# Attention scores of a hybrid decoder layer: the low product on 64 rows, two of them in two row tiles of TensorE

## The chip, the cores and the metric

The kernel runs on one core of a Trainium2 chip. A core has five engines with queues of their own: TensorE (PE in the profile; its weight loads are shown apart as PEld), VectorE (DVE), ScalarE (ACT), GpSimd (POOL) and SyncE (SP), which here only issues DMAs. TensorE multiplies a stationary operand of up to 128 rows and 128 columns with a moving operand of up to 512 columns, sums over the rows, and writes to PSUM, a memory of eight banks, each holding 512 numbers of four bytes in each of 128 partitions. The metric is the time of one execution on the device in microseconds (us), as the median of several runs.

## The reference, cut to what matters

One decoder layer over 1024 positions and 1024 channels: a norm, one wide projection, two attentions side by side, a gated merge, then a feed-forward part with a short convolution, and a last norm. The change touches only the scores of the two attentions.

```python
# differential attention: 4 heads, two score maps (c = 0, 1) of head dimension 64, causal, blocks of 128 queries
s = einsum('bqhcd,bshcd->bhcqs', q_blk, k) * scale
logits = where(dist >= 0, s - slope * dist, NEG_INF)
p = softmax(logits)
a = p[:, :, 0] - lam * p[:, :, 1]
# sliding window: 8 query heads on 2 key heads of dimension 64, a block of 128 queries sees 256 keys
s = einsum('bnqkgd,bnskd->bnkgqs', qb, kw) * d ** -0.5
p = softmax(concatenate([logits, sink], -1))[..., :-1]
```

## The kernel before, in words

All matrix products run in a rounded 32-bit type. To keep the accuracy, an operand is split into a high part (rounded) and a low part (the rest), and a product is the sum of partial products of the parts.

For the scores the head dimension is 64, half of TensorE's 128 rows, and the kernel uses the free half for the split. `q_stacks` puts q's high part and q's low part of one head on top of each other in one tile of 128 rows: the high part stands in rows 0 to 63 when c is 0, and in rows 64 to 127 when c is 1 (in the sliding window, for even and odd heads). `k_stack` makes two tiles, one with k's high part in both halves and one with k's low part in both halves. One matmul over 128 rows with the first gives high times high plus low times high; a second one, with the other tile, gives high times low plus low times low. The second is called the low product below.

The attentions are worked through in 6 units (`attention`): 4 heads of the differential attention and 2 key heads of the sliding window, each in 8 steps of 128 queries.

A differential step (`da_step`, L623 to L655) has two halves, c = 0 and 1. Each takes a score tile `sc` of two PSUM banks from a pool of two such tiles, fills it with matmuls (L636; one or two cuts of 256 to 512 keys, each with two products), and then VectorE adds the distance bias and takes the row's extreme (L640), which reads the score tile for the last time, and ScalarE takes the exponential (L641). After both halves VectorE combines the two maps (L646), TensorE transposes the result (L652), ScalarE and VectorE split it (L654, L655), and after every second step TensorE multiplies it with the values (L664 to L666).

A sliding-window step (`sw_step`) fills one `sc` tile with the scores of four heads, 256 keys each (L724): heads 0 and 1 in the tile's first bank, 2 and 3 in its second. VectorE adds the bias for each head (L727); exponentials, transposes (L745) and the product with the values (L755) follow.

Between the steps stand pieces of the wide projection that have nothing to do with attention (`back_half`: 24 matmuls of 512 columns in `mm3`, L209 to L211), placed by a table. The order on each engine isn't the order of the text: a planner goes through the program and issues, on each engine, the earliest instruction in the text whose inputs and buffers are free by its own estimate. An instruction that waits for a buffer is passed over by later ones that are ready. The order is fixed when the program is built; on the chip each engine works through its own list and waits on semaphores.

The places that the change touches are the matmul loop of `da_step` (L630 to L636) and in `sw_step` the matmul loop and the VectorE loop (L722 to L727).

Of the kernel before, what the change touches and what calls it, by code (L numbers as in the profile page):

```python
# [13 lines left out]
ALU = mybir.AluOpType  # L14
# [3 lines left out]
P = 128  # L18
D = 1024
T = 1024  # L20
# [24 lines left out]
class Trunk:  # L45
# [576 lines left out]
    def da_step(self, h, i, st, aT):  # L622
        nc, ap = self.nc, self.ap  # L623
        q, k = st
        slope = 4.0 ** -(h + 1)
        w = (i + 1) * P

        lo = P if w == 640 else 0
        cuts = ((0, 256),) if i == 0 else ((0, w),) if w <= H2 else ((0, H2 - lo), (H2 - lo, w))
        pr = []  # L630
        for c in range(2):
            sc = self.tl(self.psS, [P, T], "sc")
            qs = q[c][:, i * P:(i + 1) * P]
            for part in range(2):
                for n0, n1 in cuts:
                    nc.tensor.matmul(sc[:, lo + n0:lo + n1], qs, k[c][part][:, n0:n1], start=part == 0, stop=part == 1)  # L636
            L = self.tl(ap, [P, T], "L", bufs=4)
            s = self.tl(self.st, [P, 4], "sm", bufs=8)
            o = 896 - i * P
            nc.vector.tensor_tensor_reduce(L[:, :w], sc[:, lo:lo + w], self.bias[:, o:o + w], slope, 3e38, ALU.add, ALU.min, s[:, 0:1])  # L640
            nc.scalar.activation(L[:, :w], L[:, :w], AF.Exp, bias=s[:, 0:1], scale=-1.0, accum_out=s[:, 1:2] if c else self.s0[:, i:i + 1])  # L641
            pr.append(L)

        nc.vector.reciprocal(s[:, 2:3], s[:, 1:2])
        nc.vector.tensor_scalar(s[:, 3:4], self.s0[:, i:i + 1], s[:, 2:3], self.neglam, ALU.mult, ALU.mult)
        nc.vector.scalar_tensor_tensor(pr[0][:, :w], pr[1][:, :w], s[:, 3:4], pr[0][:, :w], ALU.mult, ALU.add)  # L646
        qo = (i % 2) * P
        for j0 in range(0, i + 1, 4):
            nj = min(4, i + 1 - j0)
            ps = self.tl(self.psT, [P, 4, P], "t")  # L650
            for j in range(nj):
                nc.tensor.transpose(ps[:, j, :], pr[0][:, (j0 + j) * P:(j0 + j + 1) * P], self.ident)  # L652
            hi, lo = aT[j0 // 4, 0], aT[j0 // 4, 1]
            nc.scalar.copy(hi[:, :nj, qo:qo + P], ps[:, :nj, :])  # L654
            nc.vector.tensor_tensor(lo[:, :nj, qo:qo + P], ps[:, :nj, :], hi[:, :nj, qo:qo + P].bitcast(F32), ALU.subtract)  # L655
# [57 lines left out]
    def sw_step(self, g, n, st):  # L713
        nc, ap = self.nc, self.ap
        q, k = st
        k0 = max(n - 1, 0) * P
        w = P if n == 0 else 256
        bo = T + (P if n == 0 else 0)
        sc = self.tl(self.psS, [P, 4, 256], "sc")
        s = self.tl(self.st, [P, 4, 4], "sw", bufs=4)  # L720
        L = self.tl(ap, [P, 4, 256], "L", bufs=4)
        for h in range(4):  # L722
            for part in range(2):
                nc.tensor.matmul(sc[:, h, :], q[h][:, n * P:(n + 1) * P], k[part][:, k0:k0 + 256], start=part == 0, stop=part == 1)  # L724
        for h in range(4):
            slope = 2.0 ** -(4 * g + h + 1)
            nc.vector.tensor_tensor_reduce(L[:, h, :w], sc[:, h, :w], self.bias[:, bo:bo + w], slope, 3e38, ALU.add, ALU.min, s[:, 0, h:h + 1])  # L727
        sink = self.vecs[:, C_SINK + 4 * g:C_SINK + 4 * g + 4]
        nc.vector.tensor_tensor(s[:, 0, :], s[:, 0, :], self.nsink[:, 4 * g:4 * g + 4], ALU.min)
        nc.vector.tensor_tensor(s[:, 1, :], s[:, 0, :], sink, ALU.add)  # L730
        nc.scalar.activation(s[:, 1, :], s[:, 1, :], AF.Exp)
        for h in range(4):
            nc.scalar.activation(L[:, h, :w], L[:, h, :w], AF.Exp, bias=s[:, 0, h:h + 1], scale=-1.0, accum_out=s[:, 2, h:h + 1])
        nc.vector.tensor_tensor(s[:, 2, :], s[:, 2, :], s[:, 1, :], ALU.add)
        self.last = nc.vector.reciprocal(s[:, 3, :], s[:, 2, :])
        for h in range(4):
            eng = nc.gpsimd if h in (3,) else nc.vector
            eng.tensor_scalar(L[:, h, :w], L[:, h, :w], s[:, 3, h:h + 1], None, ALU.mult)
        po = self.tl(self.psT, [P, H2], "t")
        nblk = w // P  # L740
        parts = []
        for b in range(nblk):
            ps = self.tl(self.psT, [P, 4, P], "t")
            for h in range(4):
                nc.tensor.transpose(ps[:, h, :], L[:, h, b * P:(b + 1) * P], self.ident)  # L745
            pt = self.tl(ap, [P, 2, 4, P], "aT", F32R, bufs=5)
            hi, lo = pt[:, 0], pt[:, 1]
            nc.scalar.copy(hi, ps)
            nc.vector.tensor_tensor(lo, ps, hi.bitcast(F32), ALU.subtract)
            parts.append((hi, lo))  # L750
        for b, (hi, lo) in enumerate(parts):
            kb = k0 // P + b
            va = self.vsw[kb // 4][:, kb % 4, g]
            for m, pt in enumerate((hi, lo)):
                nc.tensor.matmul(po, va, pt, start=b == 0 and m == 0, stop=b == nblk - 1 and m == 1)  # L755
        t = self.tl(self.gpool, [P, 4, P], "g", bufs=2)[0:64]
        nc.scalar.copy(t, po[64:128].rearrange("p (h q) -> p h q", h=4))
        pv = po[0:64].rearrange("p (c e q) -> p c e q", c=2, e=2)
        tv = t.rearrange("p (c e) q -> p c e q", e=2)
        y = self.tl(ap, [P, 2, P], "ys", bufs=3)  # L760
        for e in range(2):
            nc.vector.tensor_tensor(y[64 * e:64 * e + 64], pv[:, :, e], tv[:, :, e], ALU.add)
        self.store(self.yd[4 + 2 * g:6 + 2 * g, :, n * P:(n + 1) * P].rearrange("c p q -> p c q"), y)
# [683 lines left out]
```

## Time and profile before

| | |
|---|---|
| median of 3 runs | 1341.69 us (1340.93 to 1343.33) |
| the profiled execution | 1342.84 us, of which its span is 1340.6 us |
| mean granted TensorE clock | 0.997 |
| TensorE busy | 1319.9 us in 6264 matmuls |
| TensorE weight loads | 1097.0 us in 6264 loads |
| VectorE busy | 1069.3 us |
| ScalarE busy | 621.2 us |
| score matmuls of the differential attention (L636) | 192, from 256.9 to 390.3 us |
| score matmuls of the sliding window (L724) | 128, from 390.8 to 480.8 us |

In the profile a row of the timeline is: start, duration, engine, line, operation, output and inputs by the program's names, the part of TensorE's array (128*128 is all of it), output shape, how many in a row, and in brackets how long the engine stood idle before and what ended that. A group's row ends with its busy time, the mean duration of one in ns, and the idle time before its members. In the row of a line, three durations are the least, the median and the largest. Records of matmuls overlap: a matmul's record runs until its last result is written, and the next one starts earlier.

### The profile page before, as it was taken

How to read it: one execution, taken by the hardware profiler on the slowest of the kernel's cores; microseconds unless marked ns; L12 is line 12 of the kernel's file. 1: busy time of each engine (PE TensorE's matmuls, PEld its weight loads, DVE VectorE, ACT ScalarE, POOL GpSimd, SP SyncE). 2: the span in 40 equal slices, each digit the busy share in tenths (PEclk: the TensorE clock that was granted, in tenths of full speed). 3: DMA queues.
4: the chain of work that ended last, by engine and by line, in shares of the span. 5: the costliest groups of instructions: out<-in, count | busy, mean ns of one | idle time of the engine just before them, and what ended most of it. 6: DMA issues, size and time to landing. Idle time of an engine off the chain costs nothing.

```text
span 1340.6 us, 17301 instructions
## 1 busy us (share of the span) xinstructions
PE 1319.9 (98%) x6264; PEld 1097.0 (82%) x6264; DVE 1069.3 (80%) x1605; ACT 621.2 (46%) x1019; POOL 497.0 (37%) x365
## 2 busy tenths in 40 slices
PE   8999999999999999999999999999999999999997
PEld 6888888888888777878888888888888888888787
DVE  8847775289889876465678999999999997978985
ACT  9432232276667765333444443444443444323454
POOL 0336553001102124651446555655565510215422
PEclk9999999999999999999999999999999999999998
DMA  7423443876553235334432222222222229671333
GB/s 258 145 107 143 156 158 141 246 182 186 144 135 124 97 119 203 141 110 157 126 110 95 78 95 79 94 68 90 90 85 80 85 82 337 214 263 63 112 124 126
DMA packets 63045, 182.64 MB, mean 136 GB/s; under 512 B 6896, under 2 KB 15216, under 8 KB 62960
## 3 DMA queue, kind: packets, MB, share of 16 engines
q1 hardware_dynamic: 51504, 164.13, 37.5%
q10 hardware_dynamic: 11456, 17.41, 3.6%
q8 instruction: 49, 0.80, 0.3%
q14 instruction: 36, 0.29, 0.1%
HBM read 130.66 MB, written 50.86 MB: 135 GB/s over the span
## 4 chain that ended last, share of the span: by engine, by line
PE 87%; POOL 4%; DVE 4%; DMA 3%; ACT 1%; issue 1%; POOLq 0%; SPq 0%; ACTq 0%; DVEq 0%
PE t L920 13%; PE t L921 13%; PE t L922 13%; PE g L209 3%; PE t L914 3%; PE g L210 3%; PE g L211 3%; PE sc L636 3%; PE y L1159 2%; PE d L1159 2%; DMA gr<-gd 2%; PE sc L211 2%; PE sc L209 2%; PE sc L210 2%; PE d L920 2%; PE d L921 2%
## 5 line engine op out<-in xcount | busy, mean ns | idle before, releaser
L1089 ACT ACTIVATE c<-us,vecs 128x512 f32<-128x512 f32 x80 | 61.3, 780 | 133.2 <-POOL us L1083 129.2
L1091 DVE SCALAR_TENSOR_TENSOR c<-us,vecs,c 128x512 f32<-128x512 f32 x160 | 110.4, 747 | 8.6 <-ACT c L1089 8.5
L1083 POOL TENSOR_TENSOR us<-us,rstd 128x1024 f32<-128x1024 f32 x38 | 99.7, 2643 | 4.5 <-DVE us L469 2.4
L128 DVE TENSOR_TENSOR sl<-sf,sh 128x1024 fp32r<-128x1024 f32 x62 | 87.6, 1415 | 11.5 <-ACT sh L127 11.5
L127 ACT CAST sh<-sf 128x1024 fp32r<-128x1024 f32 x62 | 63.3, 1048 | 60.2 <-PE t L921 43.7
L176 DVE TENSOR_TENSOR wl<-raw,wh 128x1024 fp32r<-128x1024 f32 (+2 forms) x46 | 55.7, 1210 | 31.8 <-ACT wh L174 20.2
L128 DVE TENSOR_TENSOR wl<-raw,wh 128x1024 fp32r<-128x1024 f32 (+1 forms) x35 | 76.3, 2180 | 3.7 <-ACT wh L127 3.6
L103 POOL TENSOR_TENSOR sf<-rv 128x512 f32<-128x512 f32 x30 | 41.3, 1378 | 100.9 <-DVE sl L128 57.8
L174 ACT CAST wh<-raw 128x1024 fp32r<-128x1024 f32 (+2 forms) x46 | 46.1, 1001 | 61.8 <-PE sc L210 30.5
L209 PE MATMUL g<-xh,wh 128*128 128x512 f32 x176 | 70.6, 401 | 0.1
L211 PE MATMUL g<-xh,wl 128*128 128x512 f32 x176 | 70.3, 400 | 0.0
L210 PE MATMUL g<-xl,wh 128*128 128x512 f32 x176 | 70.3, 399 | 0.0
L108 POOL TENSOR_TENSOR sf<-raw,rv 128x512 f32<-128x512 f32 x30 | 40.7, 1358 | 65.3 <-DVE sl L128 65.3
L619 POOL MEMSET aT<- 128x128 f32 x32 | 6.2, 206 | 151.6 <-PE t L665 101.3
L640 DVE CUSTOM_DVE_ANT_0 L<-sc,bias 128x128 f32<-128x128 f32 (+7 forms) x64 | 47.7, 751 | 17.0 <-PE sc L636 13.7
L641 ACT ACTIVATE L<-L,sm 128x128 f32<-128x128 f32 (+7 forms) x64 | 49.6, 778 | 20.0 <-DVE sm L640 17.3
L794 POOL TENSOR_TENSOR gr<-gr,rstd 128x1024 f32<-128x1024 f32 x16 | 40.6, 2540 | 42.5 <-DMA gr<-gd 42.3
L1093 ACT ACTIVATE c<-c 128x512 f32<-128x512 f32 x40 | 24.0, 599 | 60.7 <-DVE c L1091 60.7
L128 DVE TENSOR_TENSOR wl<-rv,wh 128x512 fp32r<-128x512 f32 x30 | 49.3, 1642 | 3.5 <-ACT wh L127 3.5
L636 PE MATMUL sc<-u,u 128*128 128x512 f32 (+2 forms) x192 | 49.8, 358 | 0.0
L211 PE MATMUL sc<-mh,wl 128*128 128x512 f32 x126 | 49.1, 390 | 0.5 <-DVE wl L176 0.5
L209 PE MATMUL sc<-mh,wh 128*128 128x512 f32 x126 | 49.0, 389 | 0.0
(527 smaller groups left out, 4400.3 us busy)
## 6 DMA issues: line engine op xcount, KB each, us to landing
u<-qd SPq DMA_DIRECT2D x72, 256.0 KB, 6.6
raw<-in_w_in SPq DMA_DIRECT2D x25, 512.0 KB, 4.2
raw<-in_w_up SPq DMA_DIRECT2D x23, 512.0 KB, 3.5
hr<-hd SPq DMA_DIRECT2D x46, 256.0 KB, 4.9
hd<-c SPq DMA_DIRECT2D x22, 512.0 KB, 2.6
rv<-in_w_up SPq DMA_DIRECT2D x21, 512.0 KB, 3.5
raw<-in_w_down SPq DMA_DIRECT2D x19, 512.0 KB, 4.2
gr<-gd SPq DMA_DIRECT2D x16, 512.0 KB, 3.7
```

Of the source, the lines that this page charges most:

```text
L127: i = nc.scalar.copy(hi, src)
L128: j = nc.vector.tensor_tensor(lo, src, hi.bitcast(F32), ALU.subtract)
L209: nc.tensor.matmul(ps, wh[:, kc + o, :], ah, start=first and n == 0, stop=False)
L210: nc.tensor.matmul(ps, wh[:, kc + o, :], al, start=False, stop=False)
L211: nc.tensor.matmul(ps, wl[:, kc + o, :], ah, start=False, stop=last and n == len(kcs) - 1)
L636: nc.tensor.matmul(sc[:, lo + n0:lo + n1], qs, k[c][part][:, n0:n1], start=part == 0, stop=part == 1)
L920: nc.tensor.matmul(ps, ah[:, k, :], bh, start=first and n == 0, stop=False, skip_group_check=skip)
L921: nc.tensor.matmul(ps, ah[:, k, :], bl, start=False, stop=False, skip_group_check=skip)
L922: i = nc.tensor.matmul(ps, al[:, k, :], bh, start=False, stop=last and n == len(ks) - 1, skip_group_check=skip)
L1083: (nc.vector if j == 0 else nc.gpsimd).tensor_tensor(u[:, 2:], u[:, 2:], self.rstd, ALU.mult)
L1089: nc.scalar.activation(c, u[:, o + 2:o + 2 + H2], AF.Identity, bias=self.vecs[:, C_CB + m:C_CB + m + 1], scale=col(m, 2))
L1091: nc.vector.scalar_tensor_tensor(c, u[:, o + k:o + k + H2], col(m, k), c, ALU.mult, ALU.add)
```

## The change

In both attentions the low product is taken over 64 rows only: q's high part times k's low part. Low times low is left out of the sum. The high part of c = 0 (or of an even head) stands in rows 0 to 63 and that of c = 1 (or an odd head) in rows 64 to 127, so the two low products use different halves of TensorE's rows, its row tiles; they are written one behind the other, into different PSUM banks.

For this the order of the text changes. A differential step takes both score tiles first, then writes the high products of both halves, then the low products, cut by cut, alternating between the halves; L640 and what follows come after all of them. A sliding-window step writes the high products of its four heads in the order 0, 2, 1, 3, then the low products in the order 0, 1, 2, 3. Heads 0 and 2 now share the first bank and 1 and 3 the second. Since two sums are open in one bank at once, only the first matmul of a bank carries the start flag. The number of matmuls, their columns and the work of the other engines stay as they are.

```diff
-        for c in range(2):
-            sc = self.tl(self.psS, [P, T], "sc")
-            qs = q[c][:, i * P:(i + 1) * P]
-            for part in range(2):
-                for n0, n1 in cuts:
-                    nc.tensor.matmul(sc[:, lo + n0:lo + n1], qs, k[c][part][:, n0:n1], start=part == 0, stop=part == 1)
+        scs = [self.tl(self.psS, [P, T], "sc") for _ in range(2)]
+        for c, sc in enumerate(scs):
+            for n0, n1 in cuts:
+                nc.tensor.matmul(sc[:, lo + n0:lo + n1], q[c][:, i * P:(i + 1) * P], k[c][0][:, n0:n1], start=True, stop=False)
+        for n0, n1 in cuts:
+            for c, sc in enumerate(scs):
+                rows = slice(64 * c, 64 * c + 64)
+                nc.tensor.matmul(sc[:, lo + n0:lo + n1], q[c][rows, i * P:(i + 1) * P], k[c][1][rows, n0:n1], start=False, stop=True)
+        for c, sc in enumerate(scs):
             L = self.tl(ap, [P, T], "L", bufs=4)
...
+        at = lambda h: sc[:, 2 * (h % 2) + h // 2]
+        for h in (0, 2, 1, 3):
+            nc.tensor.matmul(at(h), q[h][:, n * P:(n + 1) * P], k[0][:, k0:k0 + 256], start=h < 2, stop=False, skip_group_check=True)
         for h in range(4):
-            for part in range(2):
-                nc.tensor.matmul(sc[:, h, :], q[h][:, n * P:(n + 1) * P], k[part][:, k0:k0 + 256], start=part == 0, stop=part == 1)
+            rows = slice(64 * (h % 2), 64 * (h % 2) + 64)
+            nc.tensor.matmul(at(h), q[h][rows, n * P:(n + 1) * P], k[1][rows, k0:k0 + 256], start=False, stop=h > 1, skip_group_check=True)
...
-            nc.vector.tensor_tensor_reduce(L[:, h, :w], sc[:, h, :w], self.bias[:, bo:bo + w], slope, 3e38, ALU.add, ALU.min, s[:, 0, h:h + 1])
+            nc.vector.tensor_tensor_reduce(L[:, h, :w], at(h)[:, :w], self.bias[:, bo:bo + w], slope, 3e38, ALU.add, ALU.min, s[:, 0, h:h + 1])
```

## The prediction

> **What bounds the kernel now.** I read the profile's page first, then the busy time of three stretches, then the groups of matmuls in the stretch of the first attention, and then TensorE's timeline row by row, because the change is about which matmul stands beside which. From the page, the span, two engines and the chain that ended last:
>
> ```profile
> span 1340.6 us, 17301 instructions
> ...
> PE 1319.9 (98%) x6264; PEld 1097.0 (82%) x6264; DVE 1069.3 (80%) x1605; ACT 621.2 (46%) x1019; POOL 497.0 (37%) x365
> ...
> PE 87%; POOL 4%; DVE 4%; DMA 3%; ACT 1%; issue 1%; POOLq 0%; SPq 0%; ACTq 0%; DVEq 0%
> ```
>
> TensorE is busy for 98% of the span and 87% of the last chain is its work. The stretches are the differential attention's score matmuls (256 to 391 us), the sliding window's (391 to 484 us) and what follows:
>
> ```profile
> core 0: us, PE busy (x) PEld busy (x) DVE busy (x) ACT busy (x) POOL busy (x), PEclk, DMA share, GB/s
> 256.00:391.00 135.00, 134.92 (x832) 117.19 (x831) 110.20 (x288) 88.84 (x209) 10.64 (x32) 1.00 0.62 165
> 391.00:484.00 93.00, 91.92 (x543) 76.55 (x542) 82.23 (x305) 66.51 (x197) 15.70 (x17) 1.00 0.41 121
> ```
>
> In the first, TensorE idles 0.1 of 135 us, at a granted clock of 1.00; in the second 1.1 of 93. VectorE, at 110 and 82 us, is next but has room. So TensorE time added or saved in these stretches moves the end almost one for one: what follows is bound by TensorE too. The matmuls concerned, from the groups of the first stretch and from the line of the second attention's scores:
>
> ```profile
> L209 PE MATMUL g<-xh,wh 128*128 128x512 f32 x72 | 28.9, 401 | 0.0
> L636 PE MATMUL sc<-u,u 128*128 128x512 f32 x80 | 27.6, 409 | 0.0
> L636 PE MATMUL sc<-u,u 128*128 128x256 f32 x64 | 16.9, 299 | 0.0
> L636 PE MATMUL sc<-u,u 128*128 128x384 f32 x48 | 15.3, 352 | 0.0
> ```
>
> ```profile
> L724 PEld LDWEIGHTS sc<-u,u x128: 186/189/217, 390.5 to 480.7; 128*128 128x128 f32 x128
> L724 PE MATMUL sc<-u,u x128: 274/283/382, 390.8 to 480.8; 128*128 128x256 f32 x128
> ```
>
> "128*128" after the operation is the part of the array in use: all of it here.
>
> **What a matmul costs, and what stands beside the scores.** TensorE's timeline around the last block of the third head and the first of the fourth, and VectorE's hold on two of its weight loads:
>
> ```profile
> 351.14 0.39 PE L210 MATMUL g<-xl,wh 128*128 128x512 f32 x1
> 351.37 1.09 PE L636 MATMUL sc<-u,u 128*128 128x512 f32 x4
> 352.29 0.40 PE L211 MATMUL g<-xh,wl 128*128 128x512 f32 x1
> 352.53 1.17 PE L636 MATMUL sc<-u,u 128*128 128x512 f32 x4
> 353.53 0.39 PE L209 MATMUL g<-xh,wh 128*128 128x512 f32 x1
> 353.76 0.39 PE L210 MATMUL g<-xl,wh 128*128 128x512 f32 x1
> ...
> 356.02 0.40 PE L636 MATMUL sc<-u,u 128*128 128x256 f32 x2
> 356.25 0.40 PE L211 MATMUL g<-xh,wl 128*128 128x512 f32 x1
> ...
> 357.19 0.40 PE L209 MATMUL g<-xh,wh 128*128 128x512 f32 x1
> 357.43 0.40 PE L636 MATMUL sc<-u,u 128*128 128x256 f32 x2
> ```
>
> ```profile
> 352.49 0.77 PEld L636 LDWEIGHTS sc<-u,u 128*128 128x128 f32 x4 [0.24 <-DVE sm L640]
> ...
> 355.90 0.31 PEld L636 LDWEIGHTS sc<-u,u 128*128 128x128 f32 x2 [0.16 <-DVE sm L640]
> ```
>
> Three readings. (1) A 512-column matmul is recorded for 0.39 us, but the next starts 0.23 later (353.53 to 353.76), two of 256 take 0.23 together (356.02 to 356.25), so 0.12 each; 384 columns lie between, about 0.175. The spacing goes by columns. (2) So each matmul overlaps the one before by 0.39 - 0.23 = 0.16 us. (3) The two halves of a head (c = 0 and 1, which use the two score buffers) do not stand together: in each of these steps the first pair or four is followed by other work, and the second waits until VectorE's L640 has emptied its buffer.
>
> **The change, part by part.** Nothing is added or taken away in number: 192 and 128 score matmuls with as many weight loads, the same VectorE, ScalarE, POOL and DMA instructions. What changes is the order of the scores and the 64 rows of the low products.
>
> *Order in the differential attention.* The new text puts both high products first and then the two low ones. But the second high product still needs a buffer that VectorE empties later, while the first low product needs only what is there. The planner of this kernel issues whatever is ready; the two rows of waits above show the second half held. Counted over the timeline, the 192 matmuls stand in 77 unbroken runs, and in 31 of the 32 steps the halves are in different runs; the exception begins at 269.83:
>
> ```profile
> 256.93 0.28 PE L636 MATMUL sc<-u,u 128*128 128x256 f32 x1
> ...
> 269.83 1.12 PE L636 MATMUL sc<-u,u 128*128 128x512 f32 x4
> ...
> 389.62 1.09 PE L636 MATMUL sc<-u,u 128*128 128x512 f32 x4
> ```
>
> So I expect the low products of 31 steps to run one half at a time, without a partner in the other row tile: 62 groups, and one pair, 63.
>
> *Order in the sliding window.* One buffer holds all four heads, so a step's matmuls can stand together. They do in 7 of 16 steps, and the 128 stand in 24 runs, from one matmul at 390.77 to eight at 479.89; where not, older work cuts in, as here:
>
> ```profile
> 399.17 1.20 PE L724 MATMUL sc<-u,u 128*128 128x256 f32 x8
> 400.21 0.39 PE L209 MATMUL g<-xh,wh 128*128 128x512 f32 x1
> ...
> 410.64 0.52 PE L724 MATMUL sc<-u,u 128*128 128x256 f32 x3
> 411.00 0.40 PE L755 MATMUL t<-aT,v 128*128 128x512 f32 x1
> ```
>
> At least 16 groups of low products, 79 in all, each with a border to full-array work on either side: 158 borders. If cut-ins split the low parts as they split today's runs, there are some 99 groups (77 + 24 runs, less the few that hold high parts only).
>
> *Gain of a pair.* If two row tiles ran wholly at once, a pair would save one spacing: in the sliding window 32 pairs x 0.12 = 3.8 us; in the differential attention, were all paired, 20 x 0.23 + 12 x 0.175 + 16 x 0.12 = 8.6 us (half of the 80, 48 and 64 matmuls are low products, two to a pair). But each matmul has its own weight load, and loads set their own pace: eight transposes of 128 columns take 0.80 us to the next matmul (row below, next start 399.17), 0.10 each. Two loads in a row thus need 0.20 where two 256-column matmuls need 0.24, which leaves 0.04 a pair. I take that end, since the loads are measured and their running at once is not: 32 x 0.04 = 1.3 us, plus 0.23 for the pair at 269.83: 1.5 us.
>
> ```profile
> 398.37 1.04 PE L652 MATMUL t<-ident,L 128*128 128x128 f32 x8
> ```
>
> [...]
>
> *Price of a border.* No matmul of before uses part of the array, so no row shows a change from 128 rows to 64 and back. Bounds: zero, if it overlaps like any other; no gain, since spacing goes by columns; above, the 0.16 us of overlap lost and the weight load exposed as well. The latter is seen where TensorE had to start afresh after a wait:
>
> ```profile
> 365.15 0.19 PEld L664 LDWEIGHTS t<-aT,v 128*128 128x128 f32 x1 [0.29 <-DVE aT L655]
> ```
>
> ```profile
> 365.15 0.39 PE L664 MATMUL t<-aT,v 128*128 128x256 f32 x1
> 365.38 0.28 PE L665 MATMUL t<-aT,v 128*128 128x256 f32 x1
> ```
>
> The first takes 0.39 instead of 0.28: 0.11 for its load, so at most 0.27 a border. I take 0.16, between these ends: the overlap is recorded only between matmuls of one shape of array, so I expect it to be lost where the shape changes, the weight load still being made ahead as it is everywhere but after a wait. [...]
>
> *Bank order.* In the sliding window, L727 of head 0 used to follow the fourth matmul, and may now follow the seventh, as heads 0 and 2 share a bank: 3 x 0.12 = 0.36 us later in 16 steps, 5.8 us at most. VectorE has 11 us of idle time in that stretch to hide it; I take 0.
>
> *Sum.* 158 x 0.16 = 25.3, less 1.5 for pairs, less the 1.1 us in which TensorE idles in the sliding window and the stall may hide: +22.7 us. The profiled execution took 1342.84 us (2.2 beyond its span), 1.15 above the median of the three runs, 1341.69; the forecast on the median is 1364.4 us. Its own range, from 126 borders (four in five of them, if some steps pair) to 198: 1359 to 1371.
>
> **The rivals.**
> - *Borders cost next to nothing* (0 to 0.06 us), halves unpaired: -1.5 to +8 us, 1340 to 1350. For it: nothing in the trace shows a border. Against it: the 0.16 us overlap is seen only between matmuls of one shape of array.
> - *Pairs run at once and borders are free: faster.* This needs the halves side by side in the differential attention, that is L640 emptying both buffers before the high products. It gives 12.4 us at best; with the loads' pace 20 x 0.23 + 12 x 0.15 + 48 x 0.04 = 8.3; with some hundredths of a microsecond a border, 5: 1329 to 1337. With 48 groups (96 borders) it decides below 12.4 / 96 = 0.13 us a border; unpaired, already 3.8 / 158 = 0.02 us undoes it. Against it stand the 31 separated steps.
> - *Paired, but borders drain:* 96 x 0.16 = 15.4, less 8.3 to 12.4: +3 to +7, about 1347. The change does what it says and still loses.
> - *Drained and reloaded:* 158 x 0.27 = 42.7, less 2.6: +40, 1382; with 198 borders +51, 1393.
>
> **How the numbers follow.** Forecast 0.47; cheap borders 0.18 (half of it within noise, the rest mostly slower); paired and free 0.08; paired and drained 0.10; drained and reloaded 0.17. The range, 1341 to 1392, leaves out the paired and free case, the faster end of cheap borders and the last microseconds of the worst, about 0.14. A measurement of this kernel tells some 0.2% (2.7 us) from no change. Faster by more: 0.08 and 0.02 of cheap borders, 0.10. Within: 0.09 of cheap borders and 0.02 of paired and drained, 0.11. Slower: 0.79.
>
> **What the changed kernel's profile would show.** The low products as rows with 64*128; if step one is right, those of c = 0 and c = 1 apart with L209 to L211 or L652 between, in about 31 of 32 steps. If the price is right, the matmul after a border starts about 0.39 us after a 512-column one and not 0.23, and the first stretch grows by about 63 x 2 x 0.16 = 20 us, the second by 3 to 5, at the same count of matmuls; VectorE's busy time stays at 110 and 82 us. I would be wrong if starts across borders stay 0.23 apart, if paired rows with starts a few ns apart fill the first stretch, or if the time appears as waits of VectorE for scores instead.

## The result, and the profile after

| | before | after |
|---|---|---|
| median of the runs shown together | 1342.51 us (4 runs, 1340.93 to 1346.34) | 1379.05 us (4 runs, 1378.62 to 1384.07) |
| ratio, 95% interval | | 1.0276 (1.0244 to 1.0309) |
| profiled execution, and its span | 1342.84 us, 1340.6 us | 1378.67 us, 1376.6 us |
| start of the last score matmul, differential | 390.3 us | 419.1 us |
| start of the last score matmul, sliding window | 480.8 us | 514.3 us |

The change makes the kernel 36.5 us slower; the forecast was 22.7 slower. The last differential score comes 28.8 us later, the last sliding-window score 33.5 us, the end 36.0 us (span). So most of the loss arises in the first stretch, 4.7 us in the second, and some 2.5 us behind the last score, where nothing was changed; 1.7 of these lie in a stretch of half clock (last section).

From the page of the kernel after: span, two engines, and the chain that ended last.

```profile
span 1376.6 us, 17292 instructions
...
PE 1354.3 (98%) x6264; PEld 1098.0 (80%) x6264; DVE 1076.8 (78%) x1605; ACT 621.5 (45%) x1019; POOL 498.5 (36%) x365
...
PE 93%; DVE 3%; ACT 1%; DMA 1%; POOL 1%; issue 1%; POOLq 0%; ACTq 0%; SPq 0%; DVEq 0%
```

TensorE has as many matmuls and loads as before and is busy 34.4 us longer, which is nearly all of the loss; VectorE is busy 7.5 us longer and its share fell. The time isn't spent waiting for another engine: it is inside TensorE. The view of two stretches (columns as in the prediction: busy time of PE, PEld, DVE, ACT, POOL, granted clock, DMA share, GB/s), cut where after's two attentions end, a little behind the last scores as there:

```profile
256.00:420.00 164.00, 163.90 (x836) 119.96 (x835) 113.80 (x289) 89.39 (x207) 10.61 (x32) 0.98 0.51 137
420.00:515.50 95.50, 93.25 (x528) 72.87 (x527) 79.02 (x293) 64.52 (x191) 15.01 (x17) 1.00 0.39 113
```

The first holds 836 matmuls in 164 us where before had 832 in 135, and TensorE is still recorded busy all the time. Where the time goes is seen only row by row. This is TensorE's timeline of after around one differential step (start, duration, line, part of the array, output shape, how many):

```profile
304.71 0.42 PE L634 MATMUL sc<-u,u 128*128 128x384 f32 x1
305.06 0.44 PE L638 MATMUL sc<-u,u 64*128 64x384 f32 x1
305.43 0.50 PE L211 MATMUL g<-xh,wl 128*128 128x512 f32 x1
305.77 0.34 PE L634 MATMUL sc<-u,u 128*128 128x384 f32 x1
306.03 0.43 PE L638 MATMUL sc<-u,u 64*128 64x384 f32 x1
306.40 0.50 PE L209 MATMUL g<-xh,wh 128*128 128x512 f32 x1
306.74 0.40 PE L634 MATMUL sc<-u,u 128*128 128x512 f32 x1
```

L634 is a high product, L638 a low one ("64*128"). Each low product stands alone between matmuls over all rows, and the two halves are apart, as the prediction had it. Take the low product at 306.03. By columns it would start 0.175 after the high one at 305.77; it starts 0.26 after, so 0.09 late. The matmul behind it would start 0.175 later; it starts 0.37 later, so 0.19 late. That one has 512 columns, and its successor starts 0.34 later and not 0.23, so 0.11 more. Together some 0.39 us for one lonely low product, of two borders. The first matmul after each border is also recorded about 0.1 us longer than its like (0.50 against 0.39, 0.43 against 0.34).

The weight loads of the same stretch show what the 0.1 is:

```profile
304.68 0.19 PEld L634 LDWEIGHTS sc<-u,u 128*128 128x128 f32 x1
305.06 0.18 PEld L638 LDWEIGHTS sc<-u,u 64*128 64x128 f32 x1 [0.19 <-issue]
305.43 0.19 PEld L211 LDWEIGHTS g<-xh,wl 128*128 128x128 f32 x1 [0.19 <-issue]
305.54 0.19 PEld L634 LDWEIGHTS sc<-u,u 128*128 128x128 f32 x1
```

At a border the load starts with its matmul (305.06 and 305.06, 305.43 and 305.43), after an idle time that no engine caused. Away from it the load runs ahead: that of the L634 matmul of 305.77 starts at 305.54. So it is in all of after's trace: at its 186 borders the load starts 0 to 3 ns before its matmul, between two matmuls over all rows 223 ns before it (median). And the columns overlap the matmul before by less than elsewhere: 0.07 us at the two borders above (0.42 - 0.35 and 0.44 - 0.37), against 0.16 in before's rows (0.39 - 0.23).

Where two low products in different row tiles stand together, they start at once, 3 ns apart. From the timeline, one group of the sliding window in after (L727 high, L730 low):

```profile
425.98 0.74 PE L727 MATMUL sc<-u,u 128*128 128x256 f32 x4
426.65 0.50 PE L730 MATMUL sc<-u,u 64*128 64x256 f32 x4
427.08 0.50 PE L211 MATMUL g<-xh,wl 128*128 128x512 f32 x1
427.42 0.39 PE L209 MATMUL g<-xh,wh 128*128 128x512 f32 x1
```

Four low products of 256 columns take 0.43 us to the next start. That is 0.24, two matmuls' worth and not four, and 0.19 more. The records of such a group start 3, 220 and 3 ns apart: two matmuls in two row tiles start together, and so do their weight loads (2 to 5 ns apart in the 36 such places of after, the matmuls 1 to 5). As an estimate, the 220 ns are the 120 of 256 columns and 100 for the first loads, so of the 0.19 some 0.10 stand inside the group and 0.09 behind it.

Counted over the whole program, after has 93 groups of low products: 70 in the differential attention (47 of one matmul, 20 of two, 3 of three) and 23 in the sliding window. In 36 places two neighbours lie in different row tiles; their saved columns are worth 4.8 us. Over the 93 groups the median excess is 93 ns into a group, 191 ns out of it and 105 ns in the matmul behind: 0.39 us a group, 0.195 a border. Summed over all groups, each start counted once, with the excess inside a group and without time at half clock, it is 36.4 us, again 0.39 a group.

### The profile page after: what moved, and what is told of

It is laid out like the page before. It is cut to its first block, busy times and chain, and to the rows that moved or that the text cites. A ratio compares the mean times of both kernels' runs of the same rounds, so it can differ in the third digit from the quotient of the medians.

```text
span 1376.6 us, 17292 instructions
## 1 busy us (share of the span) xinstructions
PE 1354.3 (98%) x6264; PEld 1098.0 (80%) x6264; DVE 1076.8 (78%) x1605; ACT 621.5 (45%) x1019; POOL 498.5 (36%) x365
## 3 DMA queue, kind: packets, MB, share of 16 engines
q1 hardware_dynamic: 51504, 164.13, 36.5%
## 4 chain that ended last, share of the span: by engine, by line
PE 93%; DVE 3%; ACT 1%; DMA 1%; POOL 1%; issue 1%; POOLq 0%; ACTq 0%; SPq 0%; DVEq 0%
PE t L926 12%; PE t L927 12%; PE t L928 12%; PE g L209 4%; PE g L211 4%; PE g L210 4%; PE sc L209 3%; PE sc L211 3%; PE sc L210 3%; PE t L920 3%; PE y L1165 2%; PE d L1165 2%; PE sc L638 2%; PE d L926 2%; PE d L927 2%; PE d L928 2%
## 5 line engine op out<-in xcount | busy, mean ns | idle before, releaser
L176 DVE TENSOR_TENSOR wl<-raw,wh 128x1024 fp32r<-128x1024 f32 (+2 forms) x46 | 59.1, 1285 | 34.4 <-ACT wh L174 22.8
L209 PE MATMUL g<-xh,wh 128*128 128x512 f32 x176 | 73.7, 418 | 0.4 <-ACT g L565 0.4
L211 PE MATMUL g<-xh,wl 128*128 128x512 f32 x176 | 72.6, 412 | 0.0
L643 DVE CUSTOM_DVE_ANT_0 L<-sc,bias 128x128 f32<-128x128 f32 (+7 forms) x64 | 47.7, 753 | 22.1 <-PE sc L638 14.9
L211 PE MATMUL sc<-mh,wl 128*128 128x512 f32 x126 | 49.1, 390 | 0.0
L210 PE MATMUL sc<-ml,wh 128*128 128x512 f32 x126 | 49.0, 389 | 0.0
L209 PE MATMUL sc<-mh,wh 128*128 128x512 f32 x126 | 49.0, 389 | 0.0
```

Source lines behind the costliest of these rows:

```text
L176: self.lo = (eng or nc.vector).tensor_tensor(wl, raw, wh.bitcast(F32), ALU.subtract)
L209: nc.tensor.matmul(ps, wh[:, kc + o, :], ah, start=first and n == 0, stop=False)
L210: nc.tensor.matmul(ps, wh[:, kc + o, :], al, start=False, stop=False)
L211: nc.tensor.matmul(ps, wl[:, kc + o, :], ah, start=False, stop=last and n == len(kcs) - 1)
```

## Theories and experiments

The theory: each group of low products costs about 0.39 us, whatever is in it, because at the change from 128 rows to 64 and back TensorE overlaps the columns less (some 0.09 us each time) and doesn't load the weights ahead (some 0.105); a pair saves the columns of one matmul; the rest is the new order. The rivals: the order does it (halves wait for their buffers, pieces of projection are used up early); a 64-row matmul is itself slow, wherever it stands; VectorE's late release of a score buffer does it, and better pairing would make the change a gain.

Of the kernels below, those with 64 rows leave out low times low as the change does; the ones with 128-row low products add it again. The probes compute nothing that the result uses. Each was compared with the kernel before on the same chip, whose median there was 1342.5 to 1343.9 us.

**The order alone.** After, with both low products over all rows; the order of the text stays.

```diff
-                rows = slice(64 * c, 64 * c + 64)
+                rows = slice(0, P)
...
-            rows = slice(64 * (h % 2), 64 * (h % 2) + 64)
+            rows = slice(0, P)
```

> The order of the changed kernel, with the low products over all 128 rows as before (so low times low is in the sum again). Theory (borders): the time goes at the changes between 128 and 64 rows, about 0.39 us for each group of 64-row matmuls; there are none here, so the time is that of the kernel before, 1342.5 us, 1340 to 1346. Rival (order): the new order makes VectorE get its scores later; then most of the 36.5 us stays, 1370 or more.

Measured: 1349.53 us (1349.15 to 1350.01), +6.3; ratio 1.0045 (1.003 to 1.006). That is above the theory's range and far below the rival's: the order by itself is a minor part of the loss, but not free, as the prediction had it. The stretch from the end of the differential scores to the last product of the sliding window's values, before and then with the order alone:

```profile
390.40:498.00 107.60, 105.89 (x606) 86.36 (x605) 93.35 (x331) 75.02 (x217) 17.61 (x19) 1.00 0.40 115
```

```profile
393.20:502.00 108.80, 104.67 (x601) 85.02 (x600) 91.94 (x331) 74.65 (x217) 16.78 (x19) 1.00 0.39 113
```

TensorE idles 4.1 us there (108.80 less 104.67) instead of 1.7, with five matmuls fewer to do. In the new order the planner issues more of the projection in the first attention: 219 matmuls of L209 to L211 stand there between the first score and the last, against 209 before, and between that and the last score of the sliding window 162 against 172. Pieces that are missing there, when TensorE waits, would explain the idle time; no run shows it by itself.

**The rows alone.** Before's order, half by half, with the low products over 64 rows: 160 low matmuls in 143 groups and no pair.

```diff
+                rows = slice(64 * c, 64 * c + 64) if part else slice(0, P)
-                    nc.tensor.matmul(sc[:, lo + n0:lo + n1], qs, k[c][part][:, n0:n1], start=part == 0, stop=part == 1)
+                    nc.tensor.matmul(sc[:, lo + n0:lo + n1], qs[rows], k[c][part][rows, n0:n1], start=part == 0, stop=part == 1)
...
+                rows = slice(64 * (h % 2), 64 * (h % 2) + 64) if part else slice(0, P)
+                nc.tensor.matmul(at(h), q[h][rows, n * P:(n + 1) * P], k[part][rows, k0:k0 + 256], start=part == 0, stop=part == 1)
```

> The order of the kernel before (high and low product of one score map behind each other), with 64-row low products; in the sliding window the heads' places in the banks are those of the change. TensorE's list has the same 160 matmuls of 64 rows, but in 143 groups instead of 93, and no two row tiles side by side. Theory (borders): 143 x 0.39 = 55.8 us on 1342.5, 1398, 1392 to 1406. Rival (a 64-row matmul costs more by itself, 36.5 us / 160 = 0.23 us each): the same number of them, 1379. Rival (the row tiles side by side get in each other's way): less than the change, below 1370.

Measured: 1402.94 us (1400.46 to 1406.18), +59.7; ratio 1.0446 (1.0423 to 1.0468). With before's order and the same matmuls the loss is larger than with the change, and it goes with the number of groups: 59.7 / 143 = 0.42 us. Neither rival's time, 1379 or below 1370, is near. A step of the sliding window in this kernel, eight matmuls in which 128 and 64 rows alternate:

```profile
429.07 2.55 PE L727 MATMUL sc<-u,u 128*128 128x256 f32 x8
431.55 0.50 PE L210 MATMUL g<-xl,wh 128*128 128x512 f32 x1
```

They take 2.48 us to the next start; before's eight took 1.04 (399.17 to 400.21 in the prediction's row). Seven inner borders and the one behind them at 0.18 each make the difference.

**Forced pairs.** After, with the low products of a differential step held until its last high product has been issued: 69 groups, 67 places with two neighbours in different row tiles.

```diff
-                nc.tensor.matmul(sc[:, lo + n0:lo + n1], q[c][:, i * P:(i + 1) * P], k[c][0][:, n0:n1], start=True, stop=False)
+                high = nc.tensor.matmul(sc[:, lo + n0:lo + n1], q[c][:, i * P:(i + 1) * P], k[c][0][:, n0:n1], start=True, stop=False)
...
-                nc.tensor.matmul(sc[:, lo + n0:lo + n1], q[c][rows, i * P:(i + 1) * P], k[c][1][rows, n0:n1], start=False, stop=True)
+                with self.tc.issue_after(high.ins):
+                    nc.tensor.matmul(sc[:, lo + n0:lo + n1], q[c][rows, i * P:(i + 1) * P], k[c][1][rows, n0:n1], start=False, stop=True)
```

> The change, with the low products of a differential step held behind the high product of its second half, so that they stand side by side: 69 groups, 67 neighbours in different row tiles instead of 93 and 36. Theory (borders): 69 x 0.39 = 26.9, less one column time for each neighbour, 10.2 us: +16.7, 1359, up to 1366 if VectorE now gets its first scores late. Rival (0.23 us for each 64-row matmul): 1379. If pairing pays for its borders as the change means it to: 1342 or less.

Measured: 1372.47 us (1371.84 to 1374.29), +29.3; ratio 1.0218 (1.0203 to 1.0233). That is above the theory's range, 7.2 us less than the change's loss and far from a gain on before, though 24 groups fewer (9.4 us at 0.39) and 10.2 us of saved columns instead of 4.8 should have given 14.8. The pairs themselves are as good as they can be:

```profile
302.00 0.34 PE L634 MATMUL sc<-u,u 128*128 128x384 f32 x1
302.27 0.44 PE L639 MATMUL sc<-u,u 64*128 64x384 f32 x2
302.64 0.50 PE L211 MATMUL g<-xh,wl 128*128 128x512 f32 x1
```

Two low products of 384 columns take 0.37 us to the next start, to the hundredth what the single one at 305.06 takes in after. So the missing 7.6 us are not the pairs' price. What the order of these pairs costs is measured next.

**The order of the forced pairs alone.** The same, with 128-row low products.

```diff
-                rows = slice(64 * c, 64 * c + 64)
+                rows = slice(0, P)
...
-            rows = slice(64 * (h % 2), 64 * (h % 2) + 64)
+            rows = slice(0, P)
```

> The order of e3_paired (low products of a differential step held behind the second half's high product) with low products over 128 rows, so without a border; low times low is in the sum. It asks where the 12.6 us come from by which e3_paired was above 1359. If the wait for the second buffer makes TensorE wait and, by its idle time, lowers the clock: the 12.6 us are here too, 1354 to 1358. If the borders lower the clock: only the order's 6 us and the waits of some 3 us, 1348 to 1352.

Measured: 1360.02 us (1356.6 to 1362.21), +16.1; ratio 1.0121 (1.0102 to 1.0139). Holding both halves together costs 16 us with no border in it, 10 more than after's order does and 2 more than the upper of the two expected ranges. This is the waits of weight loads in this kernel (who waited for whom, sum, times, longest), and its first attention:

```profile
PEld sc L634 <- DVE sm L644: 6.6, 19, 1.1
```

```profile
257.00:402.00 145.00, 140.96 (x842) 118.58 (x840) 111.06 (x283) 87.13 (x204) 10.63 (x32) 1.00 0.56 148
```

TensorE now idles 4.0 us in the first attention where it idled 0.1, because the high product of the second half waits for VectorE to empty its score buffer. More projection than before is drawn forward to fill the gap: 237 of its matmuls stand among the differential scores (209 before), and only 144 are left for the sliding window's (172 before). In the second attention TensorE idles 6.0 us, against 1.7 before:

```profile
402.00:515.00 113.00, 106.96 (x593) 86.00 (x594) 93.86 (x334) 77.75 (x222) 16.78 (x19) 0.98 0.40 118
```

Between the forced pairs with 64 rows (+29.3) and with 128 (+16.1) lie 13.2 us: 69 groups less what 67 pairs save. At 0.39 a group and 10.2 of saved columns it should be 16.7; measured are (13.2 + 10.2) / 69 = 0.34 a group. The groups are not cheaper for it: start to start, their median price in the forced pairs is 0.395 us, nearly as elsewhere. What shrinks is the waiting, as the account below shows.

**One attention at a time.** The change in the sliding window only, in the differential attention only, and the order of the latter alone. For the first, `da_step` is before's; for the other two, `sw_step` is.

```diff
-        scs = [self.tl(self.psS, [P, T], "sc") for _ in range(2)]
...
+        for c in range(2):
+            sc = self.tl(self.psS, [P, T], "sc")
+            qs = q[c][:, i * P:(i + 1) * P]
+            for part in range(2):
+                for n0, n1 in cuts:
+                    nc.tensor.matmul(sc[:, lo + n0:lo + n1], qs, k[c][part][:, n0:n1], start=part == 0, stop=part == 1)
```

> The change in the sliding window alone; the differential attention as before. 25 groups, 28 neighbours in different row tiles. Theory (borders): 25 x 0.39 = 9.8, less 3.4: +6.4, 1349, 1346 to 1352. Rival (0.23 us for each of its 64 matmuls of 64 rows): +14.7, 1357. No stretch of half clock in the trace, since the one of the changed kernel lies in the differential attention.

Measured: 1348.75 us (1346.03 to 1349.44), +5.5; ratio 1.0038 (1.0025 to 1.0051). 25 groups at 0.39 less 3.4 us of saved columns make 6.4. Even where all four heads share one buffer and most of the low products pair, the change loses.

```diff
-        at = lambda h: sc[:, 2 * (h % 2) + h // 2]
-        for h in (0, 2, 1, 3):
-            nc.tensor.matmul(at(h), q[h][:, n * P:(n + 1) * P], k[0][:, k0:k0 + 256], start=h < 2, stop=False, skip_group_check=True)
...
+            for part in range(2):
+                nc.tensor.matmul(sc[:, h, :], q[h][:, n * P:(n + 1) * P], k[part][:, k0:k0 + 256], start=part == 0, stop=part == 1)
```

> The change in the differential attention alone; the sliding window as before. 70 groups of 64-row matmuls, 7 neighbours in different row tiles. Theory (borders): 70 x 0.39 = 27.3, less 1.3: +26, 1369; with 2 to 4 us more if the stretch of half clock of the changed kernel comes again, up to 1373. Rival (0.23 us for each of its 96 matmuls of 64 rows): +22, 1365.

Measured: 1370.46 us (1368.08 to 1373.44), +28.0; ratio 1.0204 (1.0179 to 1.0229). For the third, this kernel's low products are taken over 128 rows:

```diff
-                rows = slice(64 * c, 64 * c + 64)
+                rows = slice(0, P)
```

> The new order in the differential attention alone, with low products over 128 rows (low times low is in the sum); the sliding window as before. The order alone in both attentions took 6.3 us. If that is the sliding window's late first scores and a half-clock stretch: here 1343 to 1346. Rival (the differential attention's order carries it): 1348 to 1350.

Measured: 1347.22 us (1346.12 to 1348.98), +4.8; ratio 1.0034 (1.0024 to 1.0043). It fell between the two expected ranges and tells little by itself; with the one before it, the 70 groups of the differential attention cost 23.2 and 1.3 of saved columns, 0.35 each; start to start their median is 0.39.

**The price by itself.** Added matmuls in the feed-forward part, far from the attentions: before each of 118 sums of 512 columns one more matmul into the same bank, whose result the next one overwrites; over 128 rows, over 64 rows, and over 64 rows twice. The first diff shows the added matmul alone, each of the others what differs from the probe ahead of it.

```diff
+        if first and self.probe:
+            nc.tensor.matmul(ps, ah[0:128, ks[0], :], self.B[b, ks[0]][0][0:128, cols], start=True, stop=True, skip_group_check=skip)
```

> The kernel before with 118 matmuls added in the feed-forward part, far from the attentions: one of 512 columns over all 128 rows ahead of the products of 20 column pairs, into the same bank, which the product then overwrites, so nothing computed changes. Each costs its column time: 118 x 0.23 = 27 us, 1370, less where VectorE is the later one there (down to 1360).

Measured: 1370.77 us (1368.63 to 1372.93), +28.3, 0.24 each: the price of 512 columns, as the spacing says.

```diff
-            nc.tensor.matmul(ps, ah[0:128, ks[0], :], self.B[b, ks[0]][0][0:128, cols], start=True, stop=True, skip_group_check=skip)
+            nc.tensor.matmul(ps, ah[0:64, ks[0], :], self.B[b, ks[0]][0][0:64, cols], start=True, stop=True, skip_group_check=skip)
```

> The same 118 added matmuls over 64 rows, each alone between matmuls of 128 rows. Theory (borders): 118 x (0.23 + 0.39) = 73 us, that is 46 above the probe over 128 rows. Rival (0.23 us for a 64-row matmul): 27 above it. If the price were the 0.16 us of the prediction for each border: 118 x 0.32 = 38 above it.

Measured: 1417.08 us (1416.25 to 1417.49), +74.6, and 46.3 above the 128-row probe: 0.392 us for each of 118 groups. The timelines, first with 128 rows (the added matmul is L920), then with 64:

```profile
801.21 0.39 PE L925 MATMUL t<-B_3h,sl 128*128 128x512 f32 x1
801.44 0.39 PE L920 MATMUL t<-T_0h,wh 128*128 128x512 f32 x1
801.66 0.39 PE L923 MATMUL t<-T_0h,wh 128*128 128x512 f32 x1
```

```profile
802.70 0.39 PE L925 MATMUL t<-T_3h,sl 128*128 128x512 f32 x1
803.02 0.50 PE L920 MATMUL t<-T_0h,sh 64*128 64x512 f32 x1
803.45 0.50 PE L923 MATMUL t<-T_0h,sh 128*128 128x512 f32 x1
803.78 0.39 PE L924 MATMUL t<-T_0l,sh 128*128 128x512 f32 x1
804.01 0.39 PE L925 MATMUL t<-T_0h,sl 128*128 128x512 f32 x1
```

With 128 rows the starts lie 0.23 and 0.22 apart; with 64 rows 0.32, 0.43 and 0.33, and then 0.23 again. The excess of 0.09, 0.20 and 0.10 is that of the attentions, in a place without score buffers, where no wait for VectorE stands between these starts. That leaves the rivals "order" and "VectorE" only what the two order kernels show.

```diff
         if first and self.probe:
-            nc.tensor.matmul(ps, ah[0:64, ks[0], :], self.B[b, ks[0]][0][0:64, cols], start=True, stop=True, skip_group_check=skip)
+            for _ in range(2):
+                nc.tensor.matmul(ps, ah[0:64, ks[0], :], self.B[b, ks[0]][0][0:64, cols], start=True, stop=True, skip_group_check=skip)
```

> The probe over 64 rows with two such matmuls behind each other in place of one, both in rows 0 to 63: 236 added matmuls in 118 groups; nothing computed changes. Theory (price for each group, not for each matmul): 1417 + 118 x 0.23 = 1444. Rival (price for each 64-row matmul): 1417 + 118 x 0.62 = 1490.

Measured: 1447.48 us (1446.36 to 1447.9), +103.5 against the +74.6 of the single one: 28.9 more, 0.245 for each second matmul in the same row tile. That is its columns and hardly more, so the price belongs to the group, not to the 64-row matmul. In the timeline the pair and what follows:

```profile
802.66 0.73 PE L921 MATMUL t<-B_0h,wh 64*128 64x512 f32 x2
803.32 0.50 PE L924 MATMUL t<-B_0h,wh 128*128 128x512 f32 x1
```

0.66 us for the two, where the single one took 0.43: 0.23 more. That is the columns of the second one, and no time for its weight load shows beside them.

**The best place for it.** Before, with the change only in the last two steps of each differential head, whose four low products (512 columns, in step 6 one pair of 384) can make one group of two pairs, held together and issued early: 8 groups. By the numbers found, such a group saves 0.41 to 0.46 us and costs 0.39, so some 0.4 us in all could be won.

```diff
+        late = i >= 6
+        scs = [self.tl(self.psS, [P, T], "sc") for _ in range(2)] if late else []
...
+                with self.tc.issue_after(high.ins), self.tc.high_priority(2000):
+                    nc.tensor.matmul(sc[:, lo + n0:lo + n1], q[c][rows, i * P:(i + 1) * P], k[c][1][rows, n0:n1], start=False, stop=True)
```

> Row tiles only where pairs are longest: steps 6 and 7 of each head of the differential attention, with the low products held behind the second half's high product and ahead of all other work, so that each of the 8 steps has one group of four (512 and 512 or 512 and 384 columns, two row tiles side by side); all else as before. Theory (borders): 8 x 0.39 = 3.1 against 4 x (0.46 + 0.41) = 3.5 saved: no change from the borders and pairs, and up to 4 us more for the order and for the wait for the second buffer: 1342 to 1347. If pairs of this length were worth it: below 1340.

Measured: 1345.24 us (11 runs, 1343.57 to 1346.44), +1.3; ratio 1.0012 (1.0003 to 1.0021). No gain that could be measured, rather a loss of about a microsecond; its order and the clock (last section) are both large enough for that, and no run tells them apart. No version of the change beat the kernel before.

**One account for all.** In a profiled execution every matmul's time to the next start can be set against its columns (0.23, 0.18, 0.12 and 0.11 us for 512, 384, 256 and 128, the medians of before). What is more falls to the groups, to half clock, or to all other starts, most of it waiting. This is an estimate from the traces, in us against before's profiled execution (by these medians the pairs come out 0.1 to 0.2 us higher than by the rounded spacings above):

| kernel | span | groups | saved by pairs | half clock | all else |
|---|---|---|---|---|---|
| after, 93 groups | +36.0 | 36.4 | -4.9 | +4.5 | 0.0 |
| its order alone | +6.9 | | | +1.6 | +5.3 |
| rows alone, 143 groups | +59.7 | 56.6 | | +11.4 | -8.3 |
| forced pairs, 69 groups | +29.5 | 29.9 | -10.4 | +8.2 | +1.8 |
| their order alone | +17.9 | | | +2.9 | +15.0 |

A group costs 0.39 to 0.40 us in after and in the rows alone (0.43 in the forced pairs, where a few groups hold a wait; their median is 0.395). The 0.34 to 0.42 from the differences of whole times mix this with two other things: half clock adds, and the waiting is less where there are borders, as if they made TensorE late enough for its buffers to be free. The waiting that the order brings by itself, 5.3 us, is not there in after.

## Why the prediction was right, and where it missed

The sign and the place were right. The time lay in the range, 1341 to 1392, but that was drawn wide enough to hold most rivals; the forecast's own range, 1359 to 1371, was missed, and the size was 36.5 us where 22.7 were forecast. Step by step:

- **Order in the differential attention: right in kind, with fewer groups counted than there are.** The halves do stand apart, so low products run alone. But the high and the low part of one cut are often split as well, and a step of two cuts may have up to four groups: 70 groups instead of 62 and a pair, and 23 instead of 16 in the sliding window. 93 groups against 79; the second count in the prediction, 99 with cut-ins, was nearer.
- **Price of a border: the mis-sized term.** Taken was 0.16 us, the overlap of the columns lost and the weight load still made ahead. At after's borders the load is not made ahead (0 to 3 ns instead of 223): about 0.105 us of it is exposed, as in the prediction's upper end. Of the overlap only 0.09 is lost, not 0.16. Together 0.195 a border (probe: 0.392 / 2 = 0.196), between the value taken and the upper end of 0.27. Borders cost something both on entering a group (93 ns, the median in after) and on leaving it (191, and 105 in the matmul behind). Whether TensorE waits there for the last result of the matmul before can't be read: in the records 0.07 us of the overlap stays, but the ends of matmuls are modelled in them.
- **Gain of a pair: wrong end.** The prediction let two loads one after another set the pace, 0.04 us a pair of 256 columns. They start 3 ns apart, as the matmuls do, and a pair costs what a single matmul costs (0.37 us to the next start for 384 columns, in either case). With 36 pairs that saves 4.8 us instead of 1.5, which couldn't turn the sum.
- **Order as such: taken as nothing; by itself it costs 6.3 us** (4.8 for the differential attention alone), **but not in after.** VectorE's waits for scores are 14.9 us in after (L643) against 13.7 (L640), as the prediction had it. What it missed is who fills TensorE's time: of the projection, more is drawn forward into the first attention and less is left for the second. In after that wait isn't found: all starts away from groups and half clock together come out as in before. So the term's zero came true, but not for a reason that the prediction gave.
- **Half clock: no term in the sum.** It takes 4.5 us more in after's profiled execution than in before's.
- **1.1 us hidden in idle time of the sliding window: wrong.** That idle time grew, to 2.3 us (95.50 less 93.25 in the stretch quoted above).
- **Bank order: taken as 0, and nothing speaks against it.** The change in the sliding window alone costs 5.5 us where its groups and pairs make 6.4.
- **Checks.** The first stretch grew by 28.8 us (20 was said), the second by 4.7 (3 to 5, as said). The gap behind a 512-column matmul at a border was to be 0.39; it is 0.32 into 64 rows and 0.43 out of a 512-column low product, with 0.33 to the next start behind that. The halves were to be apart in 31 of 32 steps; neighbours in different row tiles stand in 7 places of after's differential attention, so it is at least 25.

The sum with terms from after's own trace is 36.4 for the groups and 4.5 for half clock, less 4.9 for the pairs: 36.0, the growth of the span. With the experiments' terms it is 6.3 for the order, 93 x 0.39 = 36.3 for the groups, less 4.8 for the pairs: 37.8, near the 36.5 measured, but partly by luck, since the order's wait isn't in after and half clock is. The same holds for the 0.38 a group that the 30.2 us between after and its order with 128 rows (36.5 less 6.3) make with the 4.8 added back: more half clock and less waiting nearly cancel in it.

Of the rivals, "drained and reloaded" (1382 us, by 0.27 us a border: 0.16 of overlap lost and 0.11 for the load) came nearest in time, with 1379 measured, and in its two parts: the second holds nearly in full, 0.105 us of the load are exposed, and the first in part, 0.09 of the 0.16 us of overlap. "Paired and free" fell on both its conditions. Its bound, 0.13 us a border, is not met by 0.195: fully paired, with 48 groups, the change would cost 48 x 0.39 = 18.7 and gain 12.4. The forced pairs came out on that side, and lost to their order as well.

## What to carry to other kernels

A matmul over 64 of TensorE's 128 rows had a price here that isn't its own but that of the two places where it meets matmuls over all rows: 0.39 us a group, as much as 870 columns of this 32-bit type (at 0.23 for 512). Two row tiles did run wholly at once (0.37 us to the next start for two matmuls of 384 columns as for one), so by these numbers it pays only if a group holds more than that in pairs, and nothing may cut into it. Before a change asks a planner for two buffers together, look for what it will put into the gap, and for what will then be missing later: with 128 rows that cost 6 us here, and 16 when the togetherness was forced.

## What the runs showed of the hardware beyond that

A stretch of half clock. The profile after has one right at the end of the first attention (columns as above; the clock is the third number from the end):

```profile
390.00:395.00 5.00, 5.00 (x36) 4.11 (x34) 1.78 (x8) 2.77 (x7) 0.72 (x5) 0.97 0.17 66
395.00:400.00 5.00, 5.00 (x14) 3.33 (x14) 2.63 (x6) 0.58 (x1) 1.66 (x2) 0.50 0.00 0
400.00:405.00 5.00, 5.00 (x27) 3.88 (x27) 2.97 (x8) 3.34 (x9) 0.20 (x1) 0.84 0.01 3
```

At a granted clock of 0.50 TensorE does 14 matmuls in 5 us, though it is recorded busy throughout. About 3.4 us are lost there, and 1.7 in another such stretch near 1296 us. The rows-alone kernel lost some 10 us in three of them between 437 and 506 us, the forced pairs 8.5 in three between 407 and 438, and the forced pairs with 128 rows 1.7 in one (403 to 407 us).

The one near 1296 us is no mark of the change. Eleven of the thirteen profiled executions have it, the probes, the change in the differential attention alone and the sliding window alone among them (for the last none was expected). It stands some 82 us before the end, in code that neither the change nor a probe touches, at the end of a wait of 2.9 us of TensorE for VectorE or up to 1.4 us behind it, and costs 1.7 us (3.4 in the probe with two matmuls). Before and the forced pairs have the same wait and no such stretch behind it.

Those in the attentions fall where borders or waits are many; but the change in the differential attention alone has the same 70 groups there and no such stretch. No run shows the cause. It doesn't touch the price of a group, which is read from starts outside these stretches. The probes have a mean clock of 0.996 in all three, as near to before's as can be, and their 0.392 hardly depends on it.
